# Block sums of the up-projection's weights: added by VectorE, or by DMA transfers in DRAM

## The chip, the cores and the metric

One core of one Trainium2 chip runs the whole program. The metric is the device time of one execution in microseconds. Before the change it is 2464.39 us, the median of 3 runs (2463.27 to 2470.26).

## The reference

Two transformer-like blocks run one after the other on 1,024 tokens of width 1,024 (with 256 context tokens beside them), all in float32. The first block projects the normed input to q, k, v and several gates, runs a gated linear attention in both directions (a scan over chunks), pools, and mixes. The second block does a neighbourhood attention, spatial gating and a convolution, and ends with a feed-forward part:

```
def _conv_ffn(h, w_up, conv_w, conv_b, w_down):
    gate, up = jnp.split(h @ w_up, 2, axis=-1)          # w_up: 1024 x 5632
    gate = _dwconv(gate, conv_w, conv_b)                # 3 taps along the tokens
    return (jax.nn.silu(gate) * up) @ w_down            # w_down: 2816 x 1024
```

The change touches `h @ w_up`. Nothing else of what is computed changes.

## The kernel before

Every float32 product is made of three TensorE products of rounded parts: a matrix is split into hi (cast by ScalarE) and lo (the rest, subtracted by VectorE), and hi*hi, hi*lo and lo*hi are added in PSUM. `wunit` makes such a pair from a weight tile of 128x1024: a load into one of two raw buffers (`wload`, on the SP queue), the cast (L212), the subtraction (L214). The pairs rotate through three buffers, so a weight is cast up to two products ahead of its use.

The up-projection goes over 22 pairs j of weight blocks, the j-th of the gate half and the j-th of the up half, 128 columns each. For each pair the product is formed by a scheme of the Strassen kind: the two weight blocks are cut in two along the rows (a11, a12 from the gate half, a21, a22 from the up half), the tokens in two halves, and seven products of half size take the place of eight. The scheme needs four sums of weight blocks: s1 = a21 + a22, s2 = s1 + a11, s3 = a11 + a21, s4 = s2 + a12. `up_weights` loads both blocks (512 KB each), lets VectorE make the four sums into the tile sm (128x2048, two buffers; `add` is L1455), and splits a22. The products of one pair stand in three steps: `up_a` (a11 and a12, unit ua), `up_b` (two units cast from sm, ub and uc) and `up_c` (the rest, then the convolution, the gate, and the store of the result, which POOL issues, L1538). From pair 3 on the order is a(j), c(j-1), b(j).

The start is written out by hand. While block 2's output projection (`out2`) ends, `up_first` runs step a of pairs 0 to 2 between its transposes, and `to_blocks` makes the token blocks N1 and N2. Then `up_early(pairs[0])` makes the sums, the unit ub and the gate's first half (gp) of pair 0; the splits of the block T3 are issued behind it (`issue_after`); then `up_b` of pair 0, `up_early(pairs[1])`, the splits of B22 and T4 behind that, and then all else.

In block 1 `gla_proj` goes over four heads: q, k (each 48 matmuls of 512 columns and more, then `rope` on ScalarE and VectorE, then a store from one of two q buffers) and v (ten blocks of tokens into one of two v buffers). Behind it comes `gla`, the scan, which first loads masks, biases (bg) and gate weights (wup), and whose `gla_out` normalises with two small POOL instructions (L1894, L1895). Later `y_phase` makes eight products, each multiplied with a loaded tile tA (two buffers) and stored to DRAM (md); between them `tick` runs pieces of matrix-vector products that VectorE makes from loaded rows (mv_raw). The pool phase follows and begins with memsets on POOL (L718).

The framework's planner orders the instructions of each engine ahead of the run by priority (the order in which the program names them) and by its own estimate of times; each engine, and each queue, then runs its list in that order. It also places the semaphores. DMAs issued by SP and by POOL are on different queues of the same 16 DMA engines.

Of the kernel before, what the change touches and what calls it, by code (L numbers as in the profile page):

```python
# [9 lines left out]
F32 = mybir.dt.float32  # L10
# [4 lines left out]
ALU = mybir.AluOpType  # L15
AX = mybir.AxisListType

P = 128
# [6 lines left out]
DK = 128  # L25
DV = 256
FF = 2816
NFF = FF // P
# [153 lines left out]
class K:  # L182
# [506 lines left out]
    def y_phase(self, up, uT):  # L689
        nc, A = self.nc, self.A  # L690
        for j in range(8):
            pm = self.mmtile()
            self.bmm(pm, self.wunit(A["wba"][j]), uT)
            t = up.tile([P, L], F32, tag="tA", name="tA")
            nc.sync.dma_start(t, self.tAd[j])
            nc.vector.scalar_tensor_tensor(out=t, in0=t, scalar=1.0, in1=pm, op0=ALU.add, op1=ALU.mult)
            nc.sync.dma_start(self.md[j], t)
            self.tick(8)

    def pool_phase(self, pb, h, pT):  # L700
        nc, A = self.nc, self.A
# [732 lines left out]
    def block_parts(self, n, ti, f, g=None):  # L1434
# [8 lines left out]
                nc.vector.tensor_tensor(out=f, in0=f, in1=b[:, 4:8, c].bitcast(F32), op=ALU.subtract)  # L1443
        self.split(*[b[:, :, c] for b in B[n]], f)

    def up_weights(self, pr):

        nc, A, fw, j = self.nc, self.A, self.fw, pr["j"]
        r0, r1 = self.wload(A["wfu"][j]), self.wload(A["wfu"][NFF + j])
        a11, a12, a21, a22 = r0[:, :512], r0[:, 512:], r1[:, :512], r1[:, 512:]  # L1450
        if "ua" not in pr:
            pr["ua"] = self.wunit(None, raw=r0)
        sm = fw.tile([P, 2048], F32, tag="sm", bufs=2, name="sm")
        s2, s1, s3, s4 = [sm[:, i * 512:(i + 1) * 512] for i in range(4)]
        add = lambda o, x, y: nc.vector.tensor_tensor(out=o, in0=x, in1=y, op=ALU.add)  # L1455
        add(s1, a21, a22)
        add(s2, s1, a11)
        add(s3, a11, a21)
        add(s4, s2, a12)
        pr["sm"] = sm  # L1460
        pr["a22"] = [fw.tile([P, 512], F32R, tag="a22" + t, bufs=2, name="a22" + t) for t in ("hi", "lo")]
        self.split(*pr["a22"], a22)
# [179 lines left out]
    def gla_proj(self, pp, h, hc, lrs, wlr):  # L1642
        nc, A = self.nc, self.A
        hhi, hlo = h
        hchi, hclo = hc
        c = {}
        pm, pc = self.mmtile(), self.atile()
        self.bmm(pm, self.wunit(None, raw=wlr), h, extra=(pc[:, :LC], hchi, hclo))
        for n in ("rope_c", "rope_s"):
            c[n] = pp.tile([P, L], F32, tag=n, name=n)  # L1650
            nc.sync.dma_start(c[n], A[n])

        for dst, src in ((lrs[:, :L], pm), (lrs[:, L:], pc[:, :LC])):
            nc.scalar.activation(dst, src, AF.Copy, scale=-1.0)
            for b in (32, 96):
                nc.vector.scalar_tensor_tensor(out=dst[b:b + 32, :], in0=src[b:b + 32, :], scalar=-1.0,
                                               in1=dst[b:b + 32, :].bitcast(F32), op0=ALU.mult, op1=ALU.subtract)
        for hd in range(NH):
            pm = self.mmtile()
            self.bmm(pm, self.wunit(A["wq"][hd]), h)  # L1660
            nc.sync.dma_start(self.qd[hd], self.rope(pp, pm, DK ** -0.5, c))
            pm, pc = self.mmtile(), self.atile()
            self.bmm(pm, self.wunit(A["wk"][hd]), h, extra=(pc[:, :LC], hchi, hclo))
            nc.sync.dma_start(self.kd[hd], self.rope(pp, pm, 1.0, c))
            kc = pp.tile([P, LC], F32, tag="kc", bufs=2, name="kc")
            nc.scalar.copy(kc, pc[:, :LC])
            nc.sync.dma_start(self.kcd[hd], kc)
            us = [self.wunit(A["wv"][hd, u]) for u in range(2)]
            v = pp.tile([P, 10, DV], F32, tag="v", bufs=2, name="v")
            for i in range(10):  # L1670
                pv = self.atile()
                if i < 8:
                    self.amm(pv[:, :DV], us, h, slice(i * P, (i + 1) * P))
                else:
                    self.amm(pv[:, :DV], us, hc, slice((i - 8) * P, (i - 7) * P))
                nc.scalar.copy(v[:, i, :], pv[:, :DV])
            nc.sync.dma_start(self.vd[hd], v)

    def rope(self, pp, ps, scale, c):
# [238 lines left out]
```

## Time and profile before

| | before |
|---|---|
| median of 3 runs | 2464.39 us |
| the profiled execution | 2467.83 us, span 2466.1 us |
| TensorE (PE) busy | 2334.1 us, 95% |
| VectorE (DVE) busy | 1536.4 us, 62% |
| ScalarE (ACT) busy | 901.2 us, 37% |
| GpSimd (POOL) busy | 255.5 us, 10% |
| DMA queue of SP (q1) | 275.67 MB, 33.9% of 16 engines |
| DMA queue of POOL (q0) | 31.46 MB, 4.7% of 16 engines |

Times are counted from the start of the span. A timeline row gives start, duration, engine, line, operation, output and inputs, and in brackets how long the engine sat idle before it and what ended that. A wait row names who waited for whom, the total, how often, and the longest. A DMA row gives packets, MB, and the time of the packets as a share of 16 engines in the stretch. Landmarks: q, k, v projections about 87 to 322 us, scan to about 545, y phase about 700 to 800, up-projection about 1,756 to 2,205, down-projection to the end.

### The profile page before, as it was taken

How to read it: one execution, taken by the hardware profiler on the slowest of the kernel's cores; microseconds unless marked ns; L12 is line 12 of the kernel's file. 1: busy time of each engine (PE TensorE's matmuls, PEld its weight loads, DVE VectorE, ACT ScalarE, POOL GpSimd, SP SyncE). 2: the span in 40 equal slices, each digit the busy share in tenths (PEclk: the TensorE clock that was granted, in tenths of full speed). 3: DMA queues.
4: the chain of work that ended last, by engine and by line, in shares of the span. 5: the costliest groups of instructions: out<-in, count | busy, mean ns of one | idle time of the engine just before them, and what ended most of it. 6: DMA issues, size and time to landing. Idle time of an engine off the chain costs nothing. (4 is left out here: it accounts for less than half of the span.)

```text
span 2466.1 us, 32636 instructions
## 1 busy us (share of the span) xinstructions
PE 2334.1 (95%) x12693; PEld 1982.2 (80%) x12693; DVE 1536.4 (62%) x2381; ACT 901.2 (37%) x1418; POOL 255.5 (10%) x423
## 2 busy tenths in 40 slices
PE   6999999998999999998999898989899999989998
PEld 5799977777988888888989777779778888868886
DVE  6523258752665567656679367965797777767663
ACT  6311157631320122215522255653543343333331
POOL 2000001110000000002200334541100000000000
PEclk8999999998999999999999999999999999999999
DMA  7222233324345343544524483644322222228451
GB/s 250 102 84 95 75 138 106 107 84 152 128 148 179 118 120 107 204 138 146 165 65 130 157 192 103 153 133 145 112 94 77 77 78 87 84 93 271 147 177 56
DMA packets 116103, 313.06 MB, mean 127 GB/s; under 512 B 18130, under 2 KB 34002, under 8 KB 114404
## 3 DMA queue, kind: packets, MB, share of 16 engines
q1 hardware_dynamic: 105188, 275.67, 33.9%
q0 software_dynamic: 8160, 31.46, 4.7%
q10 hardware_dynamic: 2592, 3.75, 0.6%
q8 instruction: 102, 1.67, 0.3%
q14 instruction: 61, 0.50, 0.1%
HBM read 241.62 MB, written 69.21 MB: 126 GB/s over the span
## 5 line engine op out<-in xcount | busy, mean ns | idle before, releaser
L212 ACT CAST w_hi<-w_raw 128x1024 fp32r<-128x1024 f32 x153 | 160.4, 1049 | 569.5 <-PE ps_mm L227 327.8
L214 DVE TENSOR_TENSOR w_lo<-w_raw,w_hi 128x1024 fp32r<-128x1024 f32 x147 | 180.1, 1226 | 288.4 <-ACT w_hi L212 285.4
L227 PE MATMUL ps_mm<-hhi,w_hi 128*128 128x512 f32 x656 | 215.2, 403 | 2.1 <-ACT gs L552 1.7
L227 PE MATMUL ps_mm<-hhi,w_lo 128*128 128x512 f32 x656 | 210.8, 398 | 0.0
L227 PE MATMUL ps_mm<-hlo,w_hi 128*128 128x512 f32 x656 | 209.8, 398 | 0.0
L227 PEld LDWEIGHTS ps_mm<-hhi,w_hi 128*128 128x128 f32 x656 | 120.3, 189 | 26.2 <-ACT gs L552 2.1
L227 PEld LDWEIGHTS ps_mm<-hlo,w_hi 128*128 128x128 f32 x656 | 120.6, 189 | 23.7
L227 PEld LDWEIGHTS ps_mm<-hhi,w_lo 128*128 128x128 f32 x656 | 120.6, 189 | 23.6
L571 DVE SCALAR_TENSOR_TENSOR mv_acc<-mv_raw,csil,mv_acc 128x512 f32<-128x512 f32 x126 | 90.6, 746 | 35.2 <-DMA mv_raw<-in_adaw 34.2
L212 ACT CAST w_hi<-sm 128x1024 fp32r<-128x1024 f32 x44 | 46.1, 1049 | 106.2 <-PE ps_mm L1471 79.8
L241 PE MATMUL ps_z<-w_hi,hhi 128*128 128x256 f32 x256 | 75.9, 297 | 7.6 <-DVEq L1729 6.5
L242 PE MATMUL ps_py<-w_lo,mixuhi 128*128 128x256 f32 x256 | 73.3, 286 | 4.5 <-DVE w_lo L214 4.4
L214 DVE TENSOR_TENSOR w_lo<-sm,w_hi 128x1024 fp32r<-128x1024 f32 x44 | 53.7, 1221 | 37.8 <-ACT w_hi L212 37.2
L1599 PE MATMUL ps_mm<-dhi,ghi 128*128 128x512 f32 x176 | 69.1, 393 | 7.9 <-ACT dhi L1582 7.9
L1030 DVE SCALAR_TENSOR_TENSOR cacc<-hp,cvw,cacc 128x1024 f32<-128x1024 f32 x60 | 75.7, 1278 | 1.0
L241 PE MATMUL ps_py<-w_hi,mhhi 128*128 128x256 f32 x256 | 73.6, 288 | 2.6 <-DVE x L793 1.9
L242 PE MATMUL ps_z<-w_lo,hhi 128*128 128x256 f32 x256 | 73.8, 288 | 0.2 <-DVE w_lo L214 0.2
L243 PE MATMUL ps_z<-w_hi,hlo 128*128 128x256 f32 x256 | 73.7, 288 | 0.0
L1271 PE MATMUL ps_po<-pT,vs 128*128 128x256 f32 (+1 forms) x352 | 65.4, 303 | 8.8 <-ACT pT L1258 5.3
L243 PE MATMUL ps_py<-w_hi,mhlo 128*128 128x256 f32 x256 | 73.3, 286 | 0.0
L242 PE MATMUL ps_py<-w_lo,mhhi 128*128 128x256 f32 x256 | 73.2, 286 | 0.0
L243 PE MATMUL ps_py<-w_hi,mixulo 128*128 128x256 f32 x256 | 72.6, 284 | 0.5 <-DVE mixulo L1292 0.5
(513 smaller groups left out, 6749.4 us busy)
## 6 DMA issues: line engine op xcount, KB each, us to landing
mv_raw<-in_adaw SPq DMA_DIRECT2D x96, 256.0 KB, 3.1
w_raw<-in_wfu SPq DMA_DIRECT2D x47, 512.0 KB, 3.5
draw<-in_wfd SPq DMA_DIRECT2D x44, 512.0 KB, 4.4
w_raw<-in_wout SPq DMA_DIRECT2D x32, 512.0 KB, 3.6
gd<-fa POOLq DMA_DIRECT2D x22, 512.0 KB, 2.9
graw<-gd SPq DMA_DIRECT2D x44, 256.0 KB, 5.3
modraw<-in_wmod SPq DMA_DIRECT2D x16, 512.0 KB, 5.5
w_raw<-in_wv SPq DMA_DIRECT2D x16, 512.0 KB, 3.6
```

What stands on the lines that cost most here:

```text
L212: nc.scalar.copy(hi, raw)
L214: eng.tensor_tensor(out=lo, in0=raw, in1=hi.bitcast(F32), op=ALU.subtract)
L227: nc.tensor.matmul(ps[:, n * 512:(n + 1) * 512], ww[:, s], hh[:, k, f * 512:(f + 1) * 512], start=st, stop=sp)
L241: nc.tensor.matmul(ps, hhi[:, k, tok], hi[:, s], start=i == 0, stop=False)
L242: nc.tensor.matmul(ps, hhi[:, k, tok], lo[:, s], start=False, stop=False)
L243: nc.tensor.matmul(ps, hlo[:, k, tok], hi[:, s], start=False, stop=i == KT - 1)
L571: nc.vector.scalar_tensor_tensor(out=a, in0=raw, scalar=s, in1=a, op0=ALU.mult, op1=ALU.add)
L1030: nc.vector.scalar_tensor_tensor(out=acc, in0=hp[:, k:k + L], scalar=cvw[:, f, k:k + 1], in1=acc, op0=ALU.mult, op1=ALU.add)
L1271: nc.tensor.matmul(po[:, qs[0] * P:(qs[-1] + 1) * P], w, d["pT"][i][:, s0:s0 + len(qs), :], start=n == 0 and i == 0, stop=n == len(blocks) ...
L1599: nc.tensor.matmul(po[i][f], x[:, s], w[:, c], start=j == 0 and n == 0, stop=j == NFF - 1 and n == 2)
```

## The change

The four sums of all 22 pairs are made in DRAM, in new DRAM tiles smd (one per pair, 128x2048), by transfers that POOL issues: a plain DRAM-to-DRAM copy of one block, then a transfer that adds another block onto it. `weight_sums` names the 176 transfers (88 copies, 88 sums, each 256 KB in rows of 2 KB) in an order in which a copy or sum that another one needs lies far ahead of it. `more_sums` issues the next n of them, behind a small POOL instruction that reads a tile just made; it is called three times a head in `gla_proj` (11 each, 132 in all) and once a product in `y_phase` (6 each, of which 44 are left to issue). `up_weights` now loads a22 (256 KB) and the finished sums (1 MB) and makes no sums; the full gate block is loaded where ua needs it, and not a second time for pairs 0 to 2.

```diff
--- before.py
+++ after.py
@@ -696,6 +696,7 @@
             nc.vector.scalar_tensor_tensor(out=t, in0=t, scalar=1.0, in1=pm, op0=ALU.add, op1=ALU.mult)
             nc.sync.dma_start(self.md[j], t)
             self.tick(8)
+            self.more_sums(6, t)
 
     def pool_phase(self, pb, h, pT):
         nc, A = self.nc, self.A
@@ -1443,20 +1444,41 @@
                 nc.vector.tensor_tensor(out=f, in0=f, in1=b[:, 4:8, c].bitcast(F32), op=ALU.subtract)
         self.split(*[b[:, :, c] for b in B[n]], f)
 
+    def weight_sums(self):
+
+        nc, A = self.nc, self.A
+        blk = lambda i, j, k: A["wfu"][i * NFF + j][:, k * 512:(k + 1) * 512]
+        self.smd = [self.dp.tile([P, 2048], F32, tag="smd%d" % j, name="smd") for j in range(NFF)]
+        part = lambda j, n: self.smd[j][:, n * 512:(n + 1) * 512]
+        S2, S1, S3, S4 = range(4)
+        for copies, sums in (([(S1, 1, 0), (S3, 1, 0)], [(S1, 1, 1), (S3, 0, 0)]), ([(S2, S1)], [(S2, 0, 0)]),
+                             ([(S4, S2)], [(S4, 0, 1)])):
+            for j in range(NFF):
+                for c in copies:
+                    src = part(j, c[1]) if len(c) == 2 else blk(c[1], j, c[2])
+                    nc.gpsimd.dma_start(part(j, c[0]), src)
+                    yield
+            for j in range(NFF):
+                for n, i, k in sums:
+                    nc.gpsimd.dma_start(part(j, n), blk(i, j, k), accum_op=ALU.add)
+                    yield
+
+    def more_sums(self, n, src):
+
+        m = self.nc.gpsimd.tensor_scalar(out=self.mark, in0=src[:, 0:1], scalar1=1.0, scalar2=0.0, op0=ALU.mult, op1=ALU.add)
+        with self.tc.issue_after(m.ins):
+            for _ in range(n):
+                next(self.ws, None)
+
     def up_weights(self, pr):
 
         nc, A, fw, j = self.nc, self.A, self.fw, pr["j"]
-        r0, r1 = self.wload(A["wfu"][j]), self.wload(A["wfu"][NFF + j])
-        a11, a12, a21, a22 = r0[:, :512], r0[:, 512:], r1[:, :512], r1[:, 512:]
         if "ua" not in pr:
-            pr["ua"] = self.wunit(None, raw=r0)
+            pr["ua"] = self.wunit(A["wfu"][j])
+        a22 = self.wp.tile([P, 1024], F32, tag="raw", bufs=2, name="w_raw")[:, :512]
+        nc.sync.dma_start(a22, A["wfu"][NFF + j][:, 512:])
         sm = fw.tile([P, 2048], F32, tag="sm", bufs=2, name="sm")
-        s2, s1, s3, s4 = [sm[:, i * 512:(i + 1) * 512] for i in range(4)]
-        add = lambda o, x, y: nc.vector.tensor_tensor(out=o, in0=x, in1=y, op=ALU.add)
-        add(s1, a21, a22)
-        add(s2, s1, a11)
-        add(s3, a11, a21)
-        add(s4, s2, a12)
+        nc.sync.dma_start(sm, self.smd[j])
         pr["sm"] = sm
         pr["a22"] = [fw.tile([P, 512], F32R, tag="a22" + t, bufs=2, name="a22" + t) for t in ("hi", "lo")]
         self.split(*pr["a22"], a22)
@@ -1644,6 +1666,8 @@
         hhi, hlo = h
         hchi, hclo = hc
         c = {}
+        self.ws = self.weight_sums()
+        self.mark = self.cp.tile([P, 1], F32, tag="mark", name="mark")
         pm, pc = self.mmtile(), self.atile()
         self.bmm(pm, self.wunit(None, raw=wlr), h, extra=(pc[:, :LC], hchi, hclo))
         for n in ("rope_c", "rope_s"):
@@ -1658,10 +1682,14 @@
         for hd in range(NH):
             pm = self.mmtile()
             self.bmm(pm, self.wunit(A["wq"][hd]), h)
-            nc.sync.dma_start(self.qd[hd], self.rope(pp, pm, DK ** -0.5, c))
+            qr = self.rope(pp, pm, DK ** -0.5, c)
+            nc.sync.dma_start(self.qd[hd], qr)
+            self.more_sums(11, qr)
             pm, pc = self.mmtile(), self.atile()
             self.bmm(pm, self.wunit(A["wk"][hd]), h, extra=(pc[:, :LC], hchi, hclo))
-            nc.sync.dma_start(self.kd[hd], self.rope(pp, pm, 1.0, c))
+            kr = self.rope(pp, pm, 1.0, c)
+            nc.sync.dma_start(self.kd[hd], kr)
+            self.more_sums(11, kr)
             kc = pp.tile([P, LC], F32, tag="kc", bufs=2, name="kc")
             nc.scalar.copy(kc, pc[:, :LC])
             nc.sync.dma_start(self.kcd[hd], kc)
@@ -1674,6 +1702,8 @@
                 else:
                     self.amm(pv[:, :DV], us, hc, slice((i - 8) * P, (i - 7) * P))
                 nc.scalar.copy(v[:, i, :], pv[:, :DV])
+                if i == 4:
+                    self.more_sums(11, v[:, i, :])
             nc.sync.dma_start(self.vd[hd], v)
 
     def rope(self, pp, ps, scale, c):
```

## Rows read from the trace of the kernel before

**Rows 1.** Stretches: us, busy PE, PEld, DVE, ACT, POOL, clock, DMA share, GB/s.
```profile
322.00:376.00 54.00, 49.23 (x235) 39.17 (x233) 35.67 (x51) 36.04 (x45) 0.00 (x0) 1.00 0.45 164
1755.00:1781.00 26.00, 20.90 (x107) 16.77 (x105) 25.48 (x45) 18.60 (x37) 3.61 (x9) 1.00 0.20 65
1781.00:1808.00 27.00, 20.62 (x75) 15.70 (x76) 26.50 (x42) 10.28 (x15) 0.00 (x0) 0.89 0.22 78
1860.00:2190.00 330.00, 330.00 (x1420) 265.59 (x1419) 234.94 (x283) 128.03 (x151) 11.18 (x51) 1.00 0.24 79
```
**Rows 2.** TensorE's waits, 1690 to 2230 us.
```profile
PE ps_mm L1599 <- ACT dhi L1582: 7.9, 1, 7.9
PE ps_mm L1471 <- DVE w_lo L214: 3.9, 1, 3.9
PE ps_mm L1471 <- DVE gp L1501: 3.6, 1, 3.6
```
**Rows 3.** Timeline of VectorE, 1740 to 1835 us.
```profile
1774.48 0.68 DVE L1455 TENSOR_TENSOR sm<-w_raw 128x512 f32<-128x512 f32 x1
...
1781.04 0.68 DVE L1501 TENSOR_TENSOR gp<-gp,ps_mm 128x512 f32<-128x512 f32 x1
...
1787.60 1.28 DVE L1455 TENSOR_TENSOR sm<-w_raw 128x512 f32<-128x512 f32 x2
...
1790.01 0.69 DVE L1455 TENSOR_TENSOR sm<-sm,w_raw 128x512 f32<-128x512 f32 x1
...
1802.57 1.22 DVE L214 TENSOR_TENSOR w_lo<-sm,w_hi 128x1024 fp32r<-128x1024 f32 x1
```
**Rows 4.** DMA queue of SP in 689-702, 122-322, 319-335 and 721-805 us, in this order.
```profile
q1 hardware_dynamic: 888, 1.62, 40.4%
...
q1 hardware_dynamic: 4080, 15.96, 22.0%
...
q1 hardware_dynamic: 1556, 5.39, 91.1%
...
q1 hardware_dynamic: 5351, 15.29, 54.5%
```
**Rows 5.** VectorE's instructions by line, 1860 to 2190 us.
```profile
L1455 DVE TENSOR_TENSOR sm<-w_raw 128x512 f32<-128x512 f32 x32 | 22.0, 688 | 8.5 <-DMA w_raw<-in_wfu 8.4
```
**Rows 6.** Timelines of POOL and, in the fourth place, of VectorE.
```profile
380.96 0.19 POOL L1894 TENSOR_SCALAR ovv<-oss 128x1 f32<-128x1 f32 x1 [297.51 <-ACT ojunk L1892]
...
800.25 0.10 POOL L718 MEMSET u<- 128x8 f32 x1 [253.97 <-PE ps_z L596]
...
1419.62 0.51 POOL L1193 DMA_DIRECT2D qs<-q2l  x1 [1.59 <-DMA qs<-q2h]
...
816.35 1.23 DVE L727 TENSOR_TENSOR sc<-u 128x1039 f32<-128x1039 f32 x1
...
1821.08 0.63 POOL L1538 DMA_DIRECT2D gd<-fa  x1 [2.39 <-DVE fa L1537]
```
**Rows 7.** Timelines of SP, ACT and DVE around the end of the projections.
```profile
297.62 0.32 SPq L1664 DMA_DIRECT2D kd<-q  x1
...
305.34 0.37 ACT L1676 COPY v<-ps_a 128x256 f32<-128x256 f32 x1 [2.51 <-PE ps_a L243]
...
329.04 0.17 DVE L1699 TENSOR_SCALAR nbg<-bg 128x8 f32<-128x8 f32 x1 [6.81 <-DMA bg<-in_bg]
...
332.71 1.04 ACT L1707 CAST wup<-wupr 128x1024 fp32r<-128x1024 f32 x1
```
**Rows 8.** DMA queues of SP and POOL, 1412 to 1424 us.
```profile
q1 hardware_dynamic: 846, 1.50, 52.9%
q0 software_dynamic: 344, 1.30, 48.4%
```
**Rows 9.** Waits around the tile q2l: what VectorE waited for, who waited.
```profile
  DMA q2l<-q2l: 5.7, 1
...
  PE ps_m L227: 4.7, 2
```

## The prediction, made before the change was run

> **What bounds the kernel now.** The page's first section comes first: TensorE is busy for 95% of the span, VectorE for 62%, so a VectorE edit pays only where TensorE waits for VectorE. Where that is, the table by stretches and TensorE's waits tell. In the steady part of the up-projection TensorE is busy for 330.00 of 330.00 us beside VectorE's 234.94 [rows 1]: the reader is to see that VectorE work taken out there buys nothing. In the 53 us ahead of it the picture is turned round: VectorE is busy for 25.48 of 26 and 26.50 of 27 us, TensorE for 20.90 and 20.62 [rows 1], and two of TensorE's waits lie in it, 3.6 us for gp and 3.9 us for a w_lo, both VectorE's; the third, 7.9 us for dhi, belongs to the down-projection [rows 2]. The timeline of VectorE shows the additions of the change (L1455) in this stretch, in line with the work that TensorE waits for [rows 3]. So the gain is one stretch of some 50 us, and the price is paid some 1,000 to 1,650 us earlier, in block 1. There the DMA tables say how full the 16 engines are: 22.0% in the q, k, v projections, 91.1% right behind them, 54.5% in the y phase [rows 4]; what stands where in time is read from the timelines of the single engines.
>
> **What it removes.** Each of 22 pairs loses four VectorE additions of 128x512. One lasts 0.68 us, but two in a row take 1.28 [rows 3], so 0.60 is the price of one more: 88 x 0.60 = 53 us of VectorE. Of the steady part's 64 the 32 of one form are 22.0 us busy [rows 5], and all 64 are worth nothing, since TensorE has no gap there. The eight of pairs 0 and 1 lie between 1774.48 and 1790.70, in the chain that ends with the w_lo at 1802.57, the one that TensorE waits 3.9 us for [rows 2 and 3]. VectorE has no gap to speak of in it, so the chain ends 8 x 0.60 = 4.8 us earlier. TensorE can follow: its own waits in the stretch come to 3.6 + 3.9 us, and the granted clock of 0.89 over 27 us [rows 1] holds another 0.11 x 27 = 3.0 us. I count 4.8, with the first four (2.4) as the lower bound, if the order of the rest puts something else in the way, and 3.6 + 3.9 + 3.0 = 10.5 as the upper, if the clock stays up and the w_lo is drawn forward. What is late next is again VectorE: the splits of T3, B22 and T4 are still in front of that w_lo, which leaves about 3 us of the second wait standing. ScalarE's casts of sm now wait for a load instead of an addition.
>
> **What it adds on SP.** A pair's loads go from 2 x 512 KB to 512 + 256 + 1024 KB. The steady part makes 17 pairs in 330 us, one in 19.4, so 768 KB more each raise 79 GB/s [rows 1] to 120, where the fullest stretch (5.39 MB in 16 us at 91.1% [rows 4]) stands for 370 when full: it hides. An sm buffer is free two pairs ahead, and a raw buffer one; behind a waiting sm load on SP stand the next pair's w_raw loads, needed a pair later. Zero; if the cover went, one 1 MB load is about 3 us.
>
> **What it adds on POOL.** 176 DMA issues and 13 marks. An issue takes 0.63 us on POOL [rows 6], so 176 x 0.63 = 111 us. POOL sat idle for 297.51 us before its first normalisation of the scan at 380.96, and for 254 us before the first memset of the pool phase at 800.25 [rows 6]; the issues fit into these two gaps. In the attention the ninth POOL transfer in a row waited for an earlier one (qs behind qs) [rows 6], so I reckon with eight in flight, and POOL stands still once eight are out. Behind it then stand the marks, each of which holds a q or tA buffer (two deep: the next but one rope is 54 us away, so this is free unless POOL is that late), later the normalisation at 380.96 and the memset at 800.25, read by VectorE at 816.35 [rows 6].
>
> **What a transfer costs the 16 engines.** No row shows DRAM to DRAM or an adding transfer. The nearest are the 256 KB loads of the y phase with 2 KB rows: 888 packets took 40.4% of 13 us on 16 engines, 84.0 engine-us, 0.095 us each [rows 4]; 128 packets on 16 engines are 0.76 us for a plain copy. A sum moves three streams (source, old value, new value) where a copy moves two: not under 0.76, not over three loads, 2.3 us; I take the middle, 1.5. The Trainium skill ("Collectives: The Full Stack", the bandwidth ceiling: the fold count) holds that an adding transfer runs at half the rate of a copy because it needs two source reads, 62.28 against 32.35 GB/s; by that a sum here would be 1.5 us too, and no run so far shows it.
>
> **Beside q, k, v (132 of the 176).** 66 copies x 0.76 + 66 sums x 1.5 = 149 us, in 200 us of which 22.0% are taken [rows 4], so 156 free: it just fits. Weights are cast two products ahead, so doubled landing times reach nobody. The end does not fit. The last head's second and third burst start with its k and its fifth v block, at 297.62 and 305.34 [rows 7]; they are 22 sums, 33 us, of which (320 - 297.6) x 0.78 = 17.5 are done when, at 320, the scan's loads begin that already keep the engines 91.1% busy for 16 us [rows 4]. The bias bg, issued just ahead of wup, lands at 329.04, and ACT casts wup at 332.71 [rows 7]; TensorE's first scan products, in a fixed order, stand behind that cast. When a POOL burst met SP's traffic in the attention, the two queues split the engines 52.9 to 48.4 [rows 8], VectorE waited 5.7 us for a store on SP and TensorE 4.7 for VectorE [rows 9]. So the 9.0 us from 320 to 329 become up to 18, bg and wup arrive at 338, and TensorE stands 338 - 332.7 = 5.3 us. At 0.76 a sum the bursts are over by 320 and it is nothing. I take 3, as the next 54 us have 4.8 us of TensorE gaps [rows 1] that can give some back. The Trainium skill ("DMA: Bandwidth & Descriptors", queues, rings and completion order) says that each engine goes round its queues packet by packet; by that SP's loads slow to half and no further. If POOL's burst came whole before SP's loads instead, they would wait for 15.5 us of sums and TensorE for 12.
>
> **Beside the y phase (the other 44).** 22 x 0.76 + 22 x 1.5 = 50 us into 84 us that are 54.5% taken [rows 4], 38 free, so 12 us run over into the pool phase, just before the reader of the memset. VectorE's loads for the matrix-vector products get slower, but TensorE has no gap there and three PSUM buffers. Zero to 4, and I take nothing.
>
> **The sum.** The profiled execution took 2467.83 us (span 2466.1, 1.7 around it); less 4.8, plus 3.0 makes 2466.0. It lies 3.4 above the median of 2464.39, so the median becomes 2462.6. About 0.3% (7.4 us) is what a measurement of this kernel can tell from no change.
>
> **The rivals.** *Hidden in block 1, and more gained* (0.25). For it: the 78% of the engines that are free there. Against: the 91.1% behind. No price gives 2464.4 - 4.8 = 2459.6; with the upper 10.5 it is 2453.9, and if the order of VectorE changes so that the first down weight's product is no longer behind the last pair, 7.9 us [rows 2] go as well: 2446. *The sums are slow and POOL is late* (0.22, slower). The place is the normalisation at 380.96. Free engine time from 122 to 381 is 259 less 22.0% of 200 and 45% of 54 [rows 1 and 4], 190 us, and eight may be in flight; (190 - 50) / 58 = 2.4 us a sum is where it decides. Above that each 0.5 us makes POOL 29 us late; ScalarE, with four buffers for its square sums, stands behind POOL, then TensorE. At 2.6 us it costs 12, at 3.0 some 35: 2472 to 2495 with the gain counted. Against it: 2.4 is just above three loads. For it: in the attention's burst a POOL packet held an engine for 48.4% of 12 us x 16 / 344 = 0.27 us [rows 8], almost three times the 0.095. *No relief* (0.08). The sm tiles lie in memory that block 2's output projection has just used; if the 1 MB loads come only when that is free, ScalarE's casts wait for them instead of for the additions: nothing gained and 3 paid is 2467.4, two loads waited for whole, 3 us each, 2473.
>
> **How the numbers follow.** My forecast, a gain with part of it paid back, has 0.45, with its own range 2457 to 2467 (from 10.5 gained and 3 paid to 2.4 gained and 5.3 paid), all of it within 0.3%. Of the first rival I put 0.19 below 2457, 0.06 within; of no relief 0.05 above 2471.8, 0.03 within. So faster 0.19, same 0.54, slower 0.27. The range for 8 in 10 runs from 2453 to 2482.
>
> **What would show it.** Right: the waits for gp and w_lo at the start of the up-projection shrink by 4 to 5 us together and the steady part stays without a gap; the scan's first wup is cast 2 to 6 us later against the end of the projections, with a new TensorE wait ahead of it; sums fill the engines to the end of the projections and past it. Wrong: waits on the normalisation or on tA (sums dearer than 2.4), no trace of sums at 320 (cheaper than 0.8), or a changed wait for dhi.

## The result and the profile after

The changed kernel takes 2484.49 us (median of 4 runs, 2481.17 to 2488.71), beside 2464.72 for the kernel before: a ratio of 1.0081, interval 1.0058 to 1.0103. It is slower by 20 us, above the forecast's range of 2453 to 2482 us. Its profiled execution has a span of 2485.2 us, 19.1 more than the one of before.

The table by stretches of the changed kernel (us, busy PE, PEld, DVE, ACT, POOL, clock, DMA share, GB/s) answers to [rows 1]:

```profile
122.00:322.00 200.00, 199.54 (x1368) 185.88 (x1367) 52.35 (x51) 37.77 (x66) 88.01 (x140) 1.00 0.98 239
322.00:376.00 54.00, 41.00 (x181) 32.31 (x180) 25.87 (x35) 28.33 (x35) 5.15 (x7) 0.94 0.63 188
...
805.00:900.00 95.00, 74.03 (x312) 61.05 (x312) 49.58 (x62) 16.05 (x17) 7.48 (x16) 0.84 0.56 148
...
1781.00:1808.00 27.00, 23.70 (x124) 19.23 (x123) 25.27 (x45) 21.61 (x43) 4.28 (x10) 1.00 0.41 147
1808.00:1835.00 27.00, 22.59 (x91) 17.72 (x90) 23.76 (x35) 10.71 (x15) 0.00 (x0) 0.94 0.27 98
...
1860.00:2190.00 330.00, 330.00 (x1426) 266.33 (x1425) 201.64 (x221) 129.20 (x154) 11.25 (x51) 1.00 0.34 121
```

The changed kernel is 27 us late when the up-projection begins, so the work that the kernel before does in 1781 to 1808 us stands for the most part in the row of 1808 to 1835.

TensorE stands still longer in two places: it is busy for 41.00 of 54 us at the start of the scan (49.23 before) and for 74.03 of 95 behind the y phase (95.00 before). Its waits there, 87 to 900 us (who waited for whom, total, times, longest):

```profile
PE ps_z L596 <- DVE mv_acc L578: 21.0, 1, 21.0
PE ps_g L1820 <- DVE wup L1738: 8.7, 1, 8.7
```

and at the up-projection, 1690 us to the end, where the waits for gp and w_lo of [rows 2] are gone and the one for dhi has stayed:

```profile
PE ps_mm L1621 <- ACT dhi L1604: 7.6, 1, 7.6
...
PE ps_mm L1493 <- ACT u L1534: 4.4, 2, 2.6
```

VectorE's instructions that both kernels have can be laid side by side in time. The changed kernel falls behind by 9.75 us between 319 and 346 (times of the kernel before) and by 10.76 and 12.20 in 737 to 774 and 774 to 815; it wins back 5.8 between 1755 and 1870, and 7.8 more in many small pieces elsewhere. 9.75 + 22.96 - 5.8 - 7.8 = 19.1, the difference of the spans.

**The scan.** DMA queues of the changed kernel in 122 to 322 and in 322 to 345 us (packets, MB, share of 16 engines), against the 22.0% of [rows 4]:

```profile
q0 software_dynamic: 13398, 32.10, 76.9%
q1 hardware_dynamic: 4032, 15.47, 20.6%
...
q0 software_dynamic: 1355, 2.46, 58.1%
q1 hardware_dynamic: 1365, 4.39, 50.9%
```

The engines are full to the end of the projections, and behind it the two queues halve them. The timelines of POOL, VectorE and ScalarE (start, duration, engine, line, operation) show the last of the projections' sums going out at 330.85, and bg and wup late, at 339.10 and 341.71 where [rows 7] has 329.04 and 332.71:

```profile
122.86 4.45 POOL L1459 DMA_DIRECT2D smd<-in_wfu  x8
129.11 0.53 POOL L1459 DMA_DIRECT2D smd<-in_wfu  x1 [1.80 <-DMA smd<-in_wfu]
...
330.85 0.81 POOL L1463 DMA_DIRECT2D smd<-in_wfu  x1 [2.23 <-DMA smd<-in_wfu]
...
339.10 0.17 DVE L1729 TENSOR_SCALAR nbg<-bg 128x8 f32<-128x8 f32 x1 [16.58 <-DMA bg<-in_bg]
...
341.71 1.04 ACT L1737 CAST wup<-wupr 128x1024 fp32r<-128x1024 f32 x1 [7.54 <-DMA wupr<-in_wup]
```

**The y phase.** DMA queues in 730 to 833 us, 93.7% together where [rows 4] has 54.5%:

```profile
q0 software_dynamic: 4708, 11.15, 51.0%
q1 hardware_dynamic: 5332, 15.21, 42.7%
```

VectorE's waits in the second half of it, in the kernel before (762 to 800 us) and in the changed one (771 to 828 us): 2.6 us for loads of the matrix-vector product have become 26.5.

```profile
DVE mv_acc L571 <- DMA mv_raw<-in_adaw: 2.6, 1, 2.6
```

```profile
DVE mv_acc L571 <- DMA mv_raw<-in_adaw: 26.5, 8, 7.4
```

The product's last step (four instructions, L578) begins at 825.61 us, 21 us later than the scan's loss alone would have it, and TensorE's next instruction in its fixed order (L596) starts when the first of the four is done. Behind the wait the granted clock is at its lower level: L596 takes 6.96 us at 0.50, where the kernel before needs 3.66.

```profile
825.61 2.48 DVE L578 TENSOR_TENSOR mv_acc<-mv_acc,mv_row 1x512 f32<-1x512 f32 x4
...
826.42 6.96 PE L596 MATMUL ps_z<-one,mv_acc 128*128 128x1 f32 x32 [20.97 <-DVE mv_acc L578]
...
826.40:833.40 7.00, 6.97 (x33) 7.00 (x34) 2.98 (x5) 0.00 (x0) 2.01 (x5) 0.50 0.55 120
```

SP's timeline shows a loop in the late loads: the md store stands in front of the next loads and waits for VectorE's tA product, which stands behind steps that wait for loads:

```profile
796.29 0.33 SPq L697 DMA_DIRECT2D md<-tA  x1
796.95 2.98 SPq L564 DMA_DIRECT2D mv_raw<-in_adaw  x3
```

### The profile page after: what moved, and what is told of

The parts are those of the page before. It is cut to its first block, busy times and chain, and to the rows that moved or that the text cites. A ratio compares the mean times of both kernels' runs of the same rounds, so it can differ in the third digit from the quotient of the medians.

```text
span 2485.2 us, 32845 instructions
## 1 busy us (share of the span) xinstructions
PE 2326.3 (94%) x12693; PEld 1982.3 (80%) x12693; DVE 1487.6 (60%) x2293; ACT 900.5 (36%) x1418; POOL 382.2 (15%) x619
## 5 line engine op out<-in xcount | busy, mean ns | idle before, releaser
L212 ACT CAST w_hi<-w_raw 128x1024 fp32r<-128x1024 f32 x153 | 160.5, 1050 | 587.1 <-PE ps_mm L227 311.9
L1463 POOL DMA_DIRECT2D smd<-in_wfu x88 | 73.0, 1198 | 44.9 <-DMA smd<-in_wfu 39.5
```

What stands on the lines that cost most here:

```text
L212: nc.scalar.copy(hi, raw)
L1463: nc.gpsimd.dma_start(part(j, n), blk(i, j, k), accum_op=ALU.add)
```

## The experiments

Every ratio is to runs of the kernel before on the same chip, with its 95% interval.

### The gain alone, and the cost alone

```diff
     def more_sums(self, n, src):
 
+        return
...
-        nc.sync.dma_start(sm, self.smd[j])
+        nc.sync.dma_start(sm.rearrange("p (k n) -> p k n", n=1024), A["wfu"][2 * j:2 * j + 2].rearrange("k p n -> p k n"))
```

> Leaves out the sums: nothing is issued beside the projections and the y phase, and sm is loaded from two weight blocks instead (1 MB). So it is the gain alone. From the two profiles: the changed kernel is 27.3 us late just before the up-projection and 20.4 us late behind its first two pairs, so the gain is 7 us and this kernel takes about 2458. By the prediction's term (eight additions, 4.8 us) 2460. Rival: the changed kernel also wins back 5 us between 850 and 1755 us (32.6 late, then 27.3); if that comes from the change and not from its lateness, this kernel takes about 2453.

Measured: 2446.67 us, 0.9931 (0.9917 to 0.9945): 17.4 below, more than the theory and its rival had. Only 6 of it lie at the up-projection (1755 to 1870 us); the rest is in pieces of 0.5 to 1.1 us between 600 and 1755, in stretches where nothing was edited.

The second kernel keeps the transfers and has `up_weights` as before:

```diff
+        r0, r1 = self.wload(A["wfu"][j]), self.wload(A["wfu"][NFF + j])
...
-        a22 = self.wp.tile([P, 1024], F32, tag="raw", bufs=2, name="w_raw")[:, :512]
...
-        nc.sync.dma_start(sm, self.smd[j])
...
+        add(s1, a21, a22)
...
```

> The cost alone: all 176 transfers are issued as in the changed kernel, but the up-projection loads both blocks and VectorE makes the sums as before. If the transfers cost what the two profiles put down to them (9.0 us at the start of the scan, 23.6 at the end of the y phase, 5 won back later), this takes 7 us more than the changed kernel, about 2491, with TensorE waits of about 9 us for wup and 21 us for the matrix-vector product. Rival: the up-projection's larger loads of sm are part of the cost; then it takes less than the changed kernel plus 7.

Measured: 2491.32 us, 1.0113 (1.0091 to 1.0135), 6.8 above the changed kernel, as expected, though the two intervals overlap. Its TensorE waits for wup and the matrix-vector product, and for gp and w_lo at the up-projection:

```profile
PE ps_z L596 <- DVE mv_acc L578: 20.0, 1, 20.0
PE ps_g L1825 <- DVE wup L1743: 9.0, 1, 9.0
...
PE ps_mm L1498 <- DVE gp L1528: 3.6, 1, 3.6
PE ps_mm L1498 <- DVE w_lo L214: 3.1, 1, 3.1
```

So the cost comes with the transfers, and no cost of the up-projection's larger loads shows.

### What a sum costs, and which place costs it

```diff
-                    nc.gpsimd.dma_start(part(j, n), blk(i, j, k), accum_op=ALU.add)
+                    nc.gpsimd.dma_start(part(j, n), blk(i, j, k))
```

> Every transfer that adds is a plain copy of the same bytes to the same place (so the sums are left out); the order of all engines is the same. Theory: the price of an adding transfer on the 16 engines (about 1.5 us against 0.8 to 1.0 for a copy) is what overfills them. Then the 132 transfers are through before 320, the wait for wup falls from 8.7 to under 2 us, the one for the matrix-vector product from 21 to under 5, and the time is 2457 to 2462. Rival: any POOL transfers beside SP's loads slow these loads to half, whatever they do; then the wait at the end of the y phase stays above 15 us and the time above 2472.

Measured: 2458.3 us, 0.9975 (0.9964 to 0.9987). The wait for wup is gone, the one for L596 is down from 21 to 6.7 us, above the bound of 5 that was named (the profile is of the fastest run, 2449.81 us). POOL's queue in this kernel, 122 to 322 us:

```profile
q0 software_dynamic: 10560, 34.61, 61.1%
```

132 copies in 0.611 x 200 = 122 us of 16 engines are 0.93 us each. In the changed kernel's 771 to 833 us, where it makes sums alone, the queue has

```profile
q0 software_dynamic: 2832, 5.16, 51.4%
```

that is 31.9 us of 16 engines for 5.16 MB, 19.7 sums of 0.262 MB: 1.62 us each, 1.7 times a copy. Nothing else differs between the two kernels, so that price turns a loss of 20 us into a gain of 6.

```diff
             self.tick(8)
-            self.more_sums(6, t)
...
-        nc.sync.dma_start(sm, self.smd[j])
+        nc.sync.dma_start(sm[:, :1536], self.smd[j][:, :1536])
+        nc.sync.dma_start(sm[:, 1536:], A["wfu"][j][:, 512:])
```

> The y phase issues no transfer: s4 is left out (its quarter of sm is loaded from the block a12), the 132 others are as in the changed kernel. If the y phase costs 23.6 us by itself, this takes 2461, with the wait for wup at 8.7 us and none for the matrix-vector product. If that wait came from the lateness of the scan (9 us) or from somewhere else, it stays and the time is above 2475. If the 5 us that the changed kernel wins back behind it belong to the lateness of the y phase, 2466.

Measured: 2462.44 us, 0.9991 (0.9982 to 1.0000): 22 us come back from the y phase, the wait for L596 is gone, and 9.0 us for wup have stayed. So the loss in the y phase does not come from the scan's lateness, which is still there.

```diff
-            nc.sync.dma_start(self.md[j], t)
+            nc.scalar.dma_start(self.md[j], t)
```

> The changed kernel with the eight md stores of the y phase issued on ScalarE's queue in place of SP's; the transfers stay. In the changed kernel SP's md store waits for VectorE's tA product, which stands behind matrix-vector steps that wait for loads, and the next loads stand behind the store on SP: a loop that holds the loads' latency (3.2 us before, 6.3 to 9.1 after). If the loop is what makes 12 us of transfers too many into 23 us of delay, the 21 us wait falls below 10 and the time below 2473. If it is the share of the engines alone, the wait stays above 16 and the time above 2478.

Measured: 2480.13 us, 1.0063 (1.0045 to 1.0080); the longest wait for L596 fell from 21.0 to 14.5:

```profile
PE ps_z L596 <- DVE mv_acc L578: 15.5, 2, 14.5
```

Between the two theories, nearer to the engines' share. The y phase loses 17.7 us here instead of 23.0, so the loop through the md store is at most about 5 of them. Even that is not clear of noise: the intervals of the two kernels overlap, and two other kernels with the store on SP lose 19.9 and 21.1 there. Nor does the run separate the loop from the queue of its own that the store now has.

### Where the rest of the gain came from

The marks' tile lies ahead of many tiles in SBUF and moves them, w_hi and w_lo among them, by 32 bytes. (That is the planner's placement; the profile shows no addresses.) Two kernels have that tile alone, the one with 4 bytes a partition, the other with 64:

```diff
         c = {}
+        self.mark = self.cp.tile([P, 1], F32, tag="mark", name="mark")     # [P, 16] in the second
+        nc.gpsimd.memset(self.mark, 0.0)
```

> The kernel before with nothing of the change but the tile that the marks write (4 bytes a partition, allocated at the same place and written once by POOL), which moves the tiles behind it in SBUF, the weight parts w_hi and w_lo among them, by 32 bytes. The kernel without transfers is 17.4 us faster than before; 7 of these lie at the up-projection, the other 10 are spread over stretches of 600 to 1755 us in pieces of 0.5 to 1.1 that all changed kernels show, the one with VectorE's additions too. If the moved tiles are their cause, this takes about 2455. Rival: they are chance of the one profile of before, and this takes 2464.

> The same with a tile of 64 bytes a partition, which moves the same tiles by 64 bytes. If what counts is the place of w_hi and w_lo within 64 bytes, the gain is gone again: 2464. If it is something that any new tile or instruction brings, 2455 as with 32 bytes.

Measured: 2457.99 us, 0.9965 (0.9952 to 0.9979) with 32 bytes, and 2464.72 us, 0.9994 (0.9985 to 1.0004) with 64. A tile that does nothing is worth 7.3 us, and the same tile in a larger size nothing. TensorE's timeline shows how: every third of a run of matmuls with the same operands, in the kernel before, with 32 and with 64 bytes.

```profile
1309.72 0.28 PE L241 MATMUL ps_py<-w_hi,h2uhi 128*128 128x256 f32 x1
...
1310.79 0.28 PE L241 MATMUL ps_py<-w_hi,h2uhi 128*128 128x256 f32 x1
```

```profile
1309.82 0.28 PE L241 MATMUL ps_py<-w_hi,h2uhi 128*128 128x256 f32 x1
...
1310.84 0.28 PE L241 MATMUL ps_py<-w_hi,h2uhi 128*128 128x256 f32 x1
```

```profile
1309.75 0.28 PE L241 MATMUL ps_py<-w_hi,h2uhi 128*128 128x256 f32 x1
...
1310.81 0.28 PE L241 MATMUL ps_py<-w_hi,h2uhi 128*128 128x256 f32 x1
```

Nine matmuls take 1.07, 1.02 and 1.06 us, at the same duration of one and the same clock: their starts lie closer together. The stretch from 1003.5 to 1050.5 us, which all eight kernels with 32 bytes that issue nothing there make in 0.85 us less, shows no change above 0.002 in the four with 64. Not every product gains: by the starts of all such runs in the three traces, three matmuls with h2uhi and h2ulo take 0.353, 0.339 and 0.352 us, those with mhhi and mhlo 0.361 in each. Which address of which operand decides was not tried.

With that known, the gain and the change can be had without it, by the same larger tile:

```diff
-        self.mark = self.cp.tile([P, 1], F32, tag="mark", name="mark")
+        self.mark = self.cp.tile([P, 16], F32, tag="mark", name="mark")[:, 0:1]
```

> The kernel without transfers (sums left out, sm loaded from two weight blocks), with the marks' tile made 64 bytes, so that w_hi and w_lo stand within 64 bytes where they stood before: the gain of the up-projection by itself. With 32 bytes it was 17.4 below before, the tile alone 7.3 below. If the two add up, this is 8 to 10 below, 2455 to 2457; by the prediction's term, 4.8 below, 2460; by the two profiles' difference at the up-projection, 7 below, 2458.

Measured: 2459.05 us, 0.9969 (0.9957 to 0.9981): the up-projection's gain by itself is 7.6 us by the ratio (4.7 to 10.6), 5.9 by the medians. With the tile's 7.3 that leaves some 2 to 4 of the 17.4 open, so that the two simply add up is not shown.

> The changed kernel, orders of all engines the same, with the marks' tile made 64 bytes: the change without the moved weight tiles. If these are worth 7 to 8 us in it too, this takes 2492; if they are worth nothing where loads are late anyway, 2484.

Measured: 2488.11 us, 1.0094 (1.0073 to 1.0115). It lies 3.6 above the changed kernel, with intervals that overlap: what the tile is worth in it stays open between the two expectations.

### Other places, and fewer transfers

In both of the next kernels `gla_proj` issues the first 110 transfers and the y phase none; the remaining 66 go elsewhere (the comments name the places).

```diff
+            if d == 1 and not robust:
+                self.more_sums(8, nb)            # scan, once a head
...
+                self.more_sums(2, z)             # pool phase, once a product
...
+            self.more_sums(3, t)                 # merge, once a product
```

> All 176 transfers, every sum right, in other places: those of the last head's second and third burst and of the y phase (66) are issued in the scan (8 a head, while POOL is idle), the pool phase (2 a product) and the merge (3 a product), none between 298 and 320 us and none in the y phase. If the two places are the whole cost, TensorE's waits for wup (8.7) and for the matrix-vector product (21) are gone and this takes what the kernel without transfers takes, 2447, at most 4 more. Rival: the sums cost wherever they meet SP's loads (the scan loads q, k and v into single buffers, the pool phase has two buffers for the matrix-vector product); then new waits come there and it is above 2455.

Measured: 2457.09 us, 0.9963 (0.9949 to 0.9978). Both waits are gone, but it is no faster than the tile alone. The rival held in part: at the merge's tail, 1050 to 1100 us, the engines are 89% full, and at that time TensorE waits 4.8 us for mhhi (0.7 before):

```profile
PE ps_py L241 <- ACT mhhi L766: 4.8, 1, 4.8
```

```diff
+                self.more_sums(1, ts[1])         # u phase, after each pair of token blocks
...
+            if j == 0:
+                self.more_sums(3, t)         # merge, first product alone; scan and pool phase as above
```

> The spread kernel with the merge nearly empty again: 110 transfers beside the projections, 32 in the scan, 16 in the u phase (one after each pair of token blocks), 16 in the pool phase, 2 in the merge. In the spread kernel the merge's tail ran at 77% and 89% of the engines and cost some 4 us against the kernel without transfers, the scan 1, the rest is within the spread of single profiles. If that holds, this takes 2449 to 2453. Rival: what the spread kernel lost (10 us against the one without transfers) is a toll of the transfers wherever they are; then 2457 again.

Measured: 2463.6 us, 0.9992 (0.9980 to 1.0005), 12 runs from 2456.96 to 2469.32: slower than both the theory and its rival had. The theory that only the merge hurt fell: the u phase and what follows it lose 2.7 and 4.4 us (603 to 645 and 690 to 737) in the profiled execution, which was the fastest of the 12; the others' traces are not there. A toll of the transfers wherever SP's loads feed a chain is what fits, but the two kernels do not prove it for each place.

The steady part gains nothing from the sums (330.00 of 330 us busy before and after), so the last two kernels make them for the first three pairs alone, with the tile of 4 and of 64 bytes:

```diff
-            for j in range(NFF):
+            for j in range(3):                       # both loops of weight_sums; calls in head 0 alone
...
+        if j < 3:
...
+            nc.sync.dma_start(sm, self.smd[j])
+        else:
...
+            add(s1, a21, a22)                        # and the other three, as before
```

> Sums in DRAM for pairs 0 to 2 alone (12 copies and 12 sums, all issued beside the first head's projections, none later); from pair 3 on VectorE makes them as before. Nothing is left out. If the whole gain lies at the up-projection's start (7.6 us by the kernel without transfers at 64 bytes) and the 24 transfers (31 us of the engines in 200 that are 78% free) cost nothing, this takes what the tile alone takes, 2458, less 7: 2449 to 2452, without waits for gp and w_lo at the start and without the 9 and 21 us in block 1. Rival: the other 19 pairs' additions also cost (the steady part shows no gap, but the kernel without transfers is at 2446.7); then 2454 or more.

> The same with the marks' tile at 64 bytes, all orders the same: the three pairs' sums without the moved weight tiles. 2457 to 2459, as the kernel without transfers at 64 bytes (2459); if the moved tiles and not the sums make the gain, 2464.

Measured: 2452.16 us, 0.9936 (0.9922 to 0.9949), and with 64 bytes 2464.07 us, 0.9980 (0.9968 to 0.9992). The first is the fastest complete kernel of the study, 14.4 us below before; some 7 to 9 are the tile's. The second missed its 2457 to 2459 and stands at the time that was named for no gain from the sums; by its ratio they still gain 5 us (2 to 8), by its medians 2.5. The first less the tile alone, each against its own runs of before, gives 7. In place the gain is smaller than with all pairs: between 1755 and 1870 us VectorE comes forward by 4.0 and 3.5 us in these two, by 5.8 and 5.5 in the changed kernel and the one without transfers at 64 bytes. At the up-projection the waits for gp and w_lo are gone in both, and those for u are 5.9 us (1.6 in the kernel before):

```profile
PE ps_mm L1503 <- ACT u L1544: 5.9, 2, 3.3
```

## Why the prediction was wrong

**The step that failed** is "Beside the y phase": "Zero to 4, and I take nothing". It cost 23.0 us. The overflow was seen ("12 us run over into the pool phase"), and with measured prices it is 18: 45.8 us of SP's own (54.5% of 84) and 22 x 0.93 + 22 x 1.62 = 56 in a stretch of 84. But it was then priced by TensorE's products, which have three PSUM buffers, and not by who needs the loads: that is the matrix-vector product, whose last step TensorE's fixed order waits for at the end of the phase. The kernel before shows no wait there, but its timelines of VectorE and TensorE show the first of the four instructions done at 795.55 and the first L596 at 798.29, 2.7 us of slack and no other cover:

```profile
794.87 2.48 DVE L578 TENSOR_TENSOR mv_acc<-mv_acc,mv_row 1x512 f32<-1x512 f32 x4
...
798.29 3.66 PE L596 MATMUL ps_z<-one,mv_acc 128*128 128x1 f32 x32
```

Of the 23.0 us, about 18.5 are L596's later start: the wait of 21.0 less that slack. Another 3.3 are a term that the prediction had nowhere: L596 at the granted clock of 0.50 behind the wait, 6.96 us for 3.66. The loop through the md store adds at most about 5, by the kernel with the store on ScalarE's queue. A rest stays open: the plain copies' 44 x 0.93 = 41 us are only 3 over the free 38, and still cost 9 us there, 3.3 of them the same slow L596.

**The start of the scan**: right in mechanism, too small in size: 9.75 us, where 3 were taken and 5.3 was the bound. The sums left over were as reckoned: 32.10 MB are 122 transfers, so 10 of 132 were left at 322, 16 us of the engines. The halving held, 58.1% to 50.9%. It held for both loads in a row: bg came at 339.1 (338 in the bound), but wup only at 341.7; taking the middle of the bound had no ground, and the 4.8 us of gaps behind it gave nothing back. By the Trainium skill ("DMA: Bandwidth & Descriptors", queues, rings and completion order) each engine goes round its queues packet by packet; the near halves of this row agree with what the prediction made of that, but while both queues were full, in 322 to 333 us, POOL's had 611 packets to SP's 394, so a turn for each packet is not shown.

**The price of a sum**: 1.62 us where 1.5 was taken, a copy 0.93 where 0.76 was. The copy was priced as 128 packets of 0.095 us; the 132 copies are 10560 packets, 80 each, of 0.186. The 132 transfers then need some 168 us in 156 free ones, where 149 "just fits" had been argued. By the rule of the Trainium skill ("Collectives: The Full Stack", the bandwidth ceiling: the fold count) an adding transfer, there a step of a collective, runs at half the rate of a copy; measured here is 1.7 times the time, in the same direction and short of 2.

**The gain** was right in place and in size. The w_lo of 1802.57 comes forward by 4.7 to 4.8 us against 1755 in the profiles of all eleven kernels that load the first pairs' sm instead of adding it, where 8 x 0.60 = 4.8 was reckoned; by 1870 it is 5.8 in the changed kernel, and the whole kernel's 7.6 (4.7 to 10.6) is not clear of that. What differs is behind it: neither of the two waits is left, where 3 us of the second were to stay, and waits of 4.4 us for u stand in their place. Of the clock about half of the 3.0 us came back: 0.94 in 1808 to 1835 for 0.89 in 1781 to 1808 before. The steady part went as forecast (330.00 of 330, 121 GB/s for 120), and the wait for dhi did not move, so the part of the first rival that took those 7.9 us fell.

**POOL** went as forecast: eight transfers out, then one at a time. An issue takes 0.53 us for a copy and 0.81 for a sum, not 0.63. POOL is through at 333, long before the normalisation at 391; with a sum under 2.4 us the second rival's place did not decide.

**Not seen at all** was that a new tile moves others in SBUF: 7.3 us gained by the tile alone. Whether it hid part of the loss is open: with the larger tile the changed kernel is 23 us slower than before, between the 20 and 27 of the two expectations.

## What to carry to other kernels

Ask of every load beside which a transfer is put who needs it last, and how many microseconds that one has to spare: a chain that shows no wait may have 3 us left. Move only the work that the bound stretch needs: 24 transfers kept a gain (2 to 8 us with the larger tile) where 176 lost 23. And before a change is credited or blamed, repeat the kernel before with the change's new tiles alone: where a tile pushes the others in SBUF, a third of a per cent can come from that.

## What the runs showed of the hardware

- With tiles moved by 32 bytes in SBUF (by the planner's placement) nine matmuls of 256 columns took 1.02 instead of 1.07 us, with 64 bytes 1.06; others, with mhhi, kept their pace. No wait, duration or clock in these rows tells of it.
- A DRAM-to-DRAM sum of 256 KB took 1.62 us of the 16 engines and 0.81 us to issue on POOL, a copy 0.93 and 0.53.
- Behind TensorE's wait of 21 us the granted clock was 0.50, and 32 matmuls of one column took 6.96 us instead of 3.66.
